# A two-layer transformer trunk in fp32: every down unit of the MLP by seven block products, added to the state unit by unit

## The chip, the cores and the metric

One NeuronCore of a Trainium2 chip runs the whole kernel as one launch. The metric is device time in microseconds (us): the median of several runs of one program. The engines run their own instruction streams in order and wait for each other through semaphores: TensorE (PE, matmuls into PSUM), VectorE (DVE) and ScalarE (ACT) for elementwise work, GpSimd (POOL) for slower elementwise work and for DMAs that add to their destination, SyncE (SP) for plain DMAs.

## The reference

The input x is 512 tokens by 1024 features. Two layers follow, each with a token mixer (attention), a squared-ReLU MLP and a gated per-layer embedding, and a norm at the end:

```python
def rmsnorm(x, g, eps=NORM_EPS):
    x32 = x.astype(jnp.float32)
    y = x32 * lax.rsqrt(jnp.mean(x32 * x32, axis=-1, keepdims=True) + eps) * g.astype(jnp.float32)
    return y.astype(x.dtype)
...
    for i in range(DEPTH):
        hn = rmsnorm(h, norm_mix_g[i])
        ...
        hn = rmsnorm(h, norm_mlp_g[i])
        u = jnp.square(jax.nn.relu(hn @ w_mlp_up[i]))
        h = h + u @ w_mlp_down[i]
        gate = jax.nn.sigmoid(rmsnorm(h, norm_ple_g[i]) @ w_ple_gate[i])
        h = h + (p[i] @ w_ple_proj[i]) * gate
    return rmsnorm(h, final_norm_g)
```

The change lies in the line `h = h + u @ w_mlp_down[i]` (4096 hidden features to 1024), and in the output at the very end.

## The kernel before, in words

The state h is kept transposed in SBUF as eight tiles of 128 features by 512 tokens, h[0] to h[7]. To keep fp32 accuracy, every factor of a matmul is split into a high part, rounded to the format fp32r, and a low part, the rest; a product is three matmuls (`mm3`): high by high, high by low, low by high (lines 138, 141, 142). The high part is a copy on ScalarE, the low part a subtraction on VectorE.

**Up blocks.** `up(ch, c)` (L711) computes 256 of the 4096 hidden features: two PSUM banks, 48 matmuls of 512 columns. From each it makes relu (L731), square (L732) and the seven sums of token and feature quarters that the products need (L737 to L741), and splits these as one tile of 128 x 1792: high part `uh` on ScalarE (L743), low part `ul` on VectorE (L744). The hidden features are worked in four chunks (NCH), each of four up blocks.

**Down units.** `down(ch, c)` (L755) multiplies one chunk (1024 hidden features) by the weights of 256 output features, the tiles h[2c] and h[2c+1]. It is a Strassen-like scheme: seven products of weight combinations with the hidden combinations, where eight would be plain. Each product is four k steps of three matmuls of 256 columns, so a unit is 84 matmuls. The weights come as four blocks A12, A22, A21, A11 of 128 x 512 (1024 KB in `raw`, two buffers). Their sums are s13 = (A21 + A22, A21 + A11) and s24 = (s13 + A11, that + A12), by VectorE (L768 to L773); in the last chunk s13 is made by two plain DMAs and one adding DMA on GpSimd (`add_up`, L749). `split` (L775) takes high and low parts into the buffers `wh` and `wl` (three of each) and, for the single block A11, into the small buffers `e`.

Of its four banks a unit adds one and a half to the state (L828, L830). The other products are summed over the chunks in tiles of their own, `sides` (copied in the first chunk, added by VectorE at L809 in the next two, added by a DMA from GpSimd at L803 in the last), and `side_sums` (L858) folds them into the state with eight additions of 128 x 256 once per output pair, in the last chunk.

**The last unit** of each layer, `down_last` (L834), is plain: for each of its two output tiles eight k steps, of which four are two matmuls of 256 columns and four one matmul of 512, times three. Before it in the program, in the last chunk, `up` makes an extra hidden tile `b12` for it (L735, L736).

**The order of the work.** Per chunk ch = 1 to 3: up(ch, 0), then down(ch-1, 0 to 3), then up(ch, 1 to 3). After that come the last chunk's units, down(3, 0 to 3). Since down(3, 0) needs the tile of up(3, 3), which is just done, its first k steps 0 to 2 are dealt ahead of k step 3: before, for its first four products (L818). When a state tile is final, `nxt.done` (L234) splits it, times the next norm's gains (L182, L183), and adds its square to a running sum (L241, L249). A scheduler fixes the order of each engine's stream from the program and its dependencies; `order(later, earlier)` adds a constraint.

**The end.** `ple_final` (L910) transposes the state back by 32 transposes on TensorE (L920), in the program ahead of the gate's products (`contract`, L945).

In the mixers GpSimd makes the low parts of weights (L126, two halves of each tile); in the MLP VectorE does (L128, and `split`).

## Time and profile before

| | |
|---|---|
| median of 3 runs | 1308.12 us |
| lowest, highest | 1306.33, 1308.19 us |
| the profiled execution: time, span | 1309.71, 1307.9 us |
| TensorE's granted clock, mean | 0.995 |
| TensorE busy | 1279.3 us (98%) |
| VectorE busy | 1005.4 us (77%) |
| ScalarE busy | 711.8 us (54%) |
| GpSimd busy | 212.0 us (16%) |
| DMA moved | 144.25 MB, mean 110 GB/s |

How to read the profile: it is one execution, and all its times are from that one. A row of a group says line, engine, operation, tile written <- tiles read, shape and count, then busy time and mean ns of one, then the idle time of that engine ahead of these instructions and what ended it. In a timeline the first number is the start and the second the length, both in us. "PE mm L138 <- ACT uh L743: 3.9, 2, 2.2" in the waits says: TensorE's matmuls of line 138 waited for ScalarE's `uh` of line 743 for 3.9 us in all, twice, at most 2.2 us. A windows row gives the window, its length and then for each engine the busy time with the count of instructions. A DMA row ends with KB and the median us from issue to landing.

### The profile page before, as it was taken

Reading aid. Unit: us, or ns where it says so; the run is one execution under the profiler, and the core shown is the slowest. Engines: PE = TensorE matmul, PEld = TensorE weight load, DVE = VectorE, ACT = ScalarE, POOL = GpSimd, SP = SyncE. Lnnn points to the kernel's source line nnn. Section 1 sums busy time; section 2 is a strip of 40 time slices with the busy share of each in tenths; the row PEclk is TensorE's granted clock in tenths of the full one; section 3 lists DMA queues with packets and bytes.
Section 4 is the critical chain, followed back from the end, with each engine's and each line's share of the span. In section 5 each row is a group of like instructions: output and inputs, shape, how many; then the busy total and the mean of one; then the engine's idle time right before and its main releaser. Section 6 shows DMA issues by size and latency. Waiting matters only on the chain.

```text
span 1307.9 us, 19332 instructions
## 1 busy us (share of the span) xinstructions
PE 1279.3 (98%) x7520; PEld 1128.1 (86%) x7520; DVE 1005.4 (77%) x1673; ACT 711.8 (54%) x1149; POOL 212.0 (16%) x184
## 2 busy tenths in 40 slices
PE   9999999999999999999999999999999999999997
PEld 7988787888998989989889888788899898997976
DVE  6788888778848869679767777887785885986876
ACT  5666768555534335355456666765553433534544
POOL 2433434310000000001024333222000000000201
PEclk9999999999999999999999999999999999999999
DMA  6421423223232222647432222212223123254741
GB/s 210 142 81 50 134 92 122 86 77 120 68 127 97 97 97 97 193 107 187 166 124 86 81 89 81 65 57 97 97 97 128 66 100 127 77 170 137 173 146 65
DMA packets 33995, 144.25 MB, mean 110 GB/s; under 512 B 3888, under 2 KB 4624, under 8 KB 21232
## 3 DMA queue, kind: packets, MB, share of 16 engines
q1 hardware_dynamic: 29680, 135.16, 30.5%
q0 software_dynamic: 4224, 7.87, 3.5%
q8 instruction: 59, 0.97, 0.3%
q14 instruction: 32, 0.26, 0.1%
HBM read 131.92 MB, written 6.37 MB: 106 GB/s over the span
## 4 chain that ended last, share of the span: by engine, by line
PE 78%; DVE 11%; ACT 6%; DMA 3%; issue 2%; SPq 0%; POOL 0%; ACTq 0%; DVEq 0%; POOLq 0%
PE mm L138 10%; PE mm L141 10%; PE mm L142 10%; PE sc L141 5%; PE sc L142 5%; PE sc L138 5%; PE pv L142 4%; PE pv L141 4%; PE pv L138 4%; PE tp L142 4%; PE tp L141 4%; PE tp L138 4%; PE pv L553 2%; PE tp L534 2%; DMA raw<-in_w_down_dram 1%
## 5 line engine op out<-in xcount | busy, mean ns | idle before, releaser
L122 ACT ACTIVATE wh<-raw 128x1024 fp32r<-128x1024 f32 (+1 forms) x156 | 160.6, 1034 | 146.5 <-PE mm L141 50.7
L126 POOL TENSOR_TENSOR wl<-raw,wh 128x512 fp32r<-128x512 f32 (+1 forms) x132 | 177.1, 1364 | 311.0 <-ACT wh L122 294.8
L138 PE MATMUL mm<-hi,wh 128*128 128x512 f32 x472 | 187.4, 397 | 0.6 <-DVE v L445 0.4
L142 PE MATMUL mm<-hi,wl 128*128 128x512 f32 x472 | 185.0, 392 | 0.1
L141 PE MATMUL mm<-lo,wh 128*128 128x512 f32 x472 | 185.1, 392 | 0.0
L128 DVE TENSOR_TENSOR wl<-raw,wh 128x1024 fp32r<-128x1024 f32 x90 | 109.7, 1221 | 46.4 <-ACT wh L122 40.8
L142 PEld LDWEIGHTS mm<-hi,wl 128*128 128x128 f32 x472 | 88.9, 188 | 20.1 <-POOL wl L126 0.5
L138 PEld LDWEIGHTS mm<-hi,wh 128*128 128x128 f32 x472 | 89.0, 188 | 17.2 <-DVE v L445 0.6
L141 PEld LDWEIGHTS mm<-lo,wh 128*128 128x128 f32 x472 | 89.1, 189 | 15.7
L753 POOL DMA_DIRECT2D s<-in_w_down_dram x4 | 4.5, 1123 | 579.3 <-DMA s<-in_w_down_dram 313.8
L528 ACT ACTIVATE e<-e,mn 128x128 f32<-128x128 f32 (+3 forms) x96 | 53.8, 561 | 65.9 <-DVE mn L525 65.5
L782 ACT ACTIVATE wh<-s 128x1024 fp32r<-128x1024 f32 x58 | 61.1, 1053 | 52.0 <-DVE s L769 14.7
L744 DVE TENSOR_TENSOR ul<-u,uh 128x1792 fp32r<-128x1792 f32 x32 | 64.8, 2024 | 30.2 <-ACT uh L743 30.1
L743 ACT ACTIVATE uh<-u 128x1792 fp32r<-128x1792 f32 x32 | 54.5, 1702 | 48.3 <-DVE u L741 48.3
L783 DVE TENSOR_TENSOR wl<-s,wh 128x1024 fp32r<-128x1024 f32 x58 | 70.8, 1221 | 12.8 <-ACT wh L782 12.3
L732 ACT ACTIVATE u<-u 128x512 f32<-128x512 f32 x64 | 39.7, 626 | 67.9 <-DVE u L731 67.6
L138 PE MATMUL sc<-hi,wh 128*128 128x512 f32 x184 | 72.0, 391 | 0.7 <-ACT hi L182 0.7
L141 PE MATMUL sc<-lo,wh 128*128 128x512 f32 x184 | 72.0, 392 | 0.6 <-DVE lo L183 0.6
L142 PE MATMUL sc<-hi,wl 128*128 128x512 f32 x184 | 71.8, 390 | 0.0
L138 PE MATMUL mm<-wh,hi 128*128 128x256 f32 (+1 forms) x216 | 63.2, 292 | 0.0
L142 PE MATMUL mm<-wh,lo 128*128 128x256 f32 (+1 forms) x216 | 63.0, 292 | 0.0
L141 PE MATMUL mm<-wl,hi 128*128 128x256 f32 (+1 forms) x216 | 62.8, 291 | 0.0
(303 smaller groups left out, 3891.8 us busy)
## 6 DMA issues: line engine op xcount, KB each, us to landing
raw<-in_w_up_dram SPq DMA_DIRECT2D x32, 1024.0 KB, 4.8
raw<-in_w_down_dram SPq DMA_DIRECT2D x32, 1024.0 KB, 4.8
raw<-in_w_in_dram SPq DMA_DIRECT2D x23, 1024.0 KB, 4.9
raw<-in_w_gate_dram SPq DMA_DIRECT2D x8, 1024.0 KB, 6.1
bias<-urow SPq DMA_DIRECT2D x24, 256.0 KB, 3.8
raw<-in_w_outa_dram SPq DMA_DIRECT2D x8, 768.0 KB, 4.2
pj<-pjd SPq DMA_DIRECT2D x16, 256.0 KB, 5.3
h<-in_xT_dram SPq DMA_DIRECT2D x8, 256.0 KB, 6.0
```

The costliest lines, as they stand in the source:

```text
L122: nc.scalar.activation(hi, src, AF.Copy)
L126: nc.gpsimd.tensor_tensor(lo[:, kx], src[:, kx], hi[:, kx].bitcast(F32), op=ALU.subtract)
L128: nc.vector.tensor_tensor(lo, src, hi.bitcast(F32), op=ALU.subtract)
L138: mm = nc.tensor.matmul(acc, lh, rh, start=start, stop=False)
L141: nc.tensor.matmul(acc, lh, rl, start=False, stop=False)
L142: nc.tensor.matmul(acc, ll, rh, start=False, stop=stop)
L528: nc.scalar.activation(e[:, 0:n], e[:, 0:n], AF.Exp, scale=-1.0, bias=mn, accum_out=s)
L732: nc.scalar.activation(ui, ui, AF.Square, scale=0.5)
L743: nc.scalar.activation(uh, u, AF.Copy)
L744: part = nc.vector.tensor_tensor(ul, u, uh.bitcast(F32), op=ALU.subtract)
L782: nc.scalar.activation(hi, src, AF.Copy)
L783: low[:] = [nc.vector.tensor_tensor(lo, src, hi.bitcast(F32), op=ALU.subtract).ins]
```

## The change

Every down unit, the last of a layer included, now runs the seven products, and each adds its results to the state itself; the side tiles, `b12`, `down_last`, `finished` and `side_sums` are gone. The block order in memory becomes A12, A22, A11, A21. In every unit s13 is made by two plain DMAs and an adding DMA, the raw load brings three blocks (768 KB), and GpSimd makes S2 = s13[0] + A11 and s4 = S2 + A12 (one 128 x 512 addition each). Three tiles of 128 x 1024 are split, and s4 in `e` tiles. The results come in four banks: ScalarE copies the first (L783), and eight VectorE additions (L794 to L802), four of 512 and four of 256 columns, put everything into h[2c] and h[2c+1]. In the last chunk's first unit all seven products do k steps 0 to 2 before k step 3. In the final stage the transposes are a function of the half, `turn(0)` and `turn(1)`, called after the products of blocks 1 and 2.

```diff
         def up(ch, c):
...
-            part = nc.vector.tensor_tensor(ul, u, uh.bitcast(F32), op=ALU.subtract)
-            hidden[ch, c] = (uh, ul, part.ins)
-
-        A12, A22, A21, A11 = range(4)
+            nc.vector.tensor_tensor(ul, u, uh.bitcast(F32), op=ALU.subtract)
+            hidden[ch, c] = (uh, ul, t4.ins)
+
+        A12, A22, A11, A21 = range(4)
+        S2 = A21
+
+        def halves(src, pool, tag, bufs):
+            n = src.shape[1]
+            hi, lo = (pool.tile([P, n, 4, P], F32R, tag=t, name=nm(t), bufs=b) for t, b in zip(tag, bufs))
+            src = src.rearrange("p s (k c) -> p s k c", k=4)
+            nc.scalar.activation(hi, src, AF.Copy)
+            return hi, lo, nc.vector.tensor_tensor(lo, src, hi.bitcast(F32), op=ALU.subtract).ins
+
+        def factors(src, late=None):
             sv = src.rearrange("p (s c) -> p s c", s=4)
+            s13 = fpool.tile([P, 2, S], F32, tag="s13", name=nm("s13"), bufs=2)
             for x in range(2):
                 nc.sync.dma_start(s13[:, x], sv[:, A21])
-            nc.gpsimd.dma_start(s13, sv[:, A22:A11 + 1:2], accum_op=ALU.add)
...
+            nc.gpsimd.dma_start(s13, sv[:, A22:A11 + 1], accum_op=ALU.add)
+            raw = wpool.tile([P, 4, S], F32, tag="raw", name=nm("raw"), bufs=2)
+            nc.sync.dma_start(raw[:, 0:3], sv[:, 0:3])
+            s4 = fpool.tile([P, 1, S], F32, tag="s4", name=nm("s4"), bufs=1)
+            nc.gpsimd.tensor_tensor(raw[:, S2], s13[:, 0], raw[:, A11], op=ALU.add)
+            nc.gpsimd.tensor_tensor(s4[:, 0], raw[:, S2], raw[:, A12], op=ALU.add)
+            w = ("wh", "wl")
+            w13 = halves(s13, wpool, w, (3, 3))
+            w12 = halves(raw[:, A11:S2 + 1], wpool, w, (3, 3))
+            wa2 = halves(raw[:, A12:A22 + 1], wpool, w, (3, 3))
+            w4 = halves(s4, spool, ("e", "e"), (T_BUFS["e"],) * 2)
+            if late is not None:
+                order(wa2[2], late)
+                order(w4[2], late)
+            return [(w12, 0, B11), (w13, 0, T1), (w12, 1, T2), (w13, 1, T3), (wa2, 0, B21), (w4, 0, B22), (wa2, 1, T4)]
+
+        def products(ws, us, head=False):
             banks = [ps_wide() for _ in range(4)]
-
-            def product(bank, half, w, x, t, start, stop, ks=range(4)):
-                wh, wl = w
+            t = spool.tile([P, S], F32, tag="e", name=nm("xw"), bufs=T_BUFS["e"])
+            places = [(0, 0), (0, 1), (1, 0), (1, 1), (2, 0), (2, 1), (3, 0)]
...
+            for ks in ((0, 1, 2), (3,)) if head else (range(4),):
+                for p in (0, 1, 3, 2, 4, 5, 6):
+                    product(p, ks)
+            nc.scalar.activation(t, banks[0], AF.Copy)
+            return banks, t
+
+        def down(ch, c):
+            last = ch == NCH - 1
+            head = last and c == 0
+            ws = factors(w_down[layer, 4 * ch + c], hidden[ch, 3][2] if head else None)
+            banks, t = products(ws, [hidden[ch, k] for k in range(4)], head)
+            left, right = slice(0, HW), slice(HW, S)
+            h1, h2 = h[2 * c], h[2 * c + 1]
+            x, w = t[:, left], t[:, right]
+            nc.vector.tensor_tensor(h1, h1, banks[0], op=ALU.add)
+            nc.vector.tensor_tensor(t, t, banks[1], op=ALU.add)
+            nc.vector.tensor_tensor(h2[:, left], h2[:, left], banks[1][:, right], op=ALU.subtract)
+            nc.vector.tensor_tensor(h1[:, right], h1[:, right], x, op=ALU.add)
+            h2v = h2.rearrange("p (a c) -> p a c", a=2)
+            nc.vector.tensor_tensor(h2v, h2v, t[:, None, left].to_broadcast([P, 2, HW]), op=ALU.subtract)
+            nc.vector.tensor_tensor(h2[:, right], h2[:, right], w, op=ALU.subtract)
+            nc.vector.tensor_tensor(h1, h1, banks[2], op=ALU.add)
+            nc.vector.tensor_tensor(h2[:, left], h2[:, left], banks[3][:, left], op=ALU.subtract)
             if last:
...
+                for i in range(2):
+                    nxt.done(2 * c + i)
...
-        side_sums(3)
-        for c in range(3):
+        for c in range(4):
             down(NCH - 1, c)
-        down_last(3)
...
                     if b == 1:
+                        turn(0)
+                    if b == 2:
                         rcol = tok_cols(norm.finish())
+                        turn(1)
```

What this makes of VectorE's stream where the first down unit of a chunk ends and the second begins (third round of layer 0). Before: `ul` (L744) is the hidden tile's low part, `wl` and `e` (L783) are low parts of weights, L809 adds to a side tile, L828 and L830 to the state.

```order
L744 TENSOR_TENSOR ul_4944<-u_4941,uh_4943 128x1792
L783 TENSOR_TENSOR wl_5085<-s_913_5074,wh_5084 128x1024
L828 TENSOR_TENSOR h_93<-h_93,tp_4966 128x512
L830 TENSOR_TENSOR h_94<-h_94,tp_4967 128x256
L783 TENSOR_TENSOR wl_5089<-s_914_5075,wh_5088 128x1024
L783 TENSOR_TENSOR wl_5159<-raw_5072,wh_5158 128x1024
```

The second unit's first low part stands ahead of the two state additions of the first unit, its second low part behind them. After, at the same place (L730 is now the hidden tile's low part, L741 a weight's, L794 to L802 add to the state):

```order
L730 TENSOR_TENSOR ul_4991<-u_4989,uh_4990 128x1792
L795 TENSOR_TENSOR xw_5030<-xw_5030,sc_5027 128x512
L796 TENSOR_TENSOR h_94<-h_94,sc_5027 128x256
L797 TENSOR_TENSOR h_93<-h_93,xw_5030 128x256
L799 TENSOR_TENSOR h_94<-h_94,xw_5030 128x512
L801 TENSOR_TENSOR h_93<-h_93,tp_5028 128x512
L800 TENSOR_TENSOR h_94<-h_94,xw_5030 128x256
L802 TENSOR_TENSOR h_94<-h_94,tp_5029 128x256
L741 TENSOR_TENSOR wl_5134<-s_912_5124,wh_5133 128x1024
L741 TENSOR_TENSOR wl_5138<-raw_5128,wh_5137 128x1024
L741 TENSOR_TENSOR wl_5142<-raw_5128,wh_5141 128x1024
```

All three wide low parts of the second unit now stand behind the last state addition of the first, which reads the bank `tp_5029` of the first unit's last product. TensorE's stream at the same place, after (pv_5149 to mm_5152 are the second unit's banks):

```order
L138 MATMUL pv_5149<-uh_4210,wh_5137 128x256
L141 MATMUL pv_5149<-ul_4211,wh_5137 128x256
L138 MATMUL pv_5150<-uh_4210,wh_5133 128x256
L141 MATMUL pv_5150<-ul_4211,wh_5133 128x256
L138 MATMUL mm_5151<-uh_4210,wh_5141 128x256
L141 MATMUL mm_5151<-ul_4211,wh_5141 128x256
L138 MATMUL mm_5152<-uh_4210,wh_5141 128x256
L141 MATMUL mm_5152<-ul_4211,wh_5141 128x256
L142 MATMUL pv_5150<-uh_4210,wl_5134 128x256
```

Eight matmuls that need only high parts come first, and the ninth reads the low part `wl_5134`. In the last chunk of layer 0, where its first unit ends and its second begins, VectorE's stream before (L865 folds a side tile, L183 is the low part of a final state tile, L773 makes a weight sum):

```order
L783 TENSOR_TENSOR wl_5785<-stage_5482,wh_5784 128x1024
L828 TENSOR_TENSOR h_93<-h_93,sc_5666 128x512
L830 TENSOR_TENSOR h_94<-h_94,sc_5667 128x256
L783 TENSOR_TENSOR wl_5789<-s_1006_5777,wh_5788 128x1024
L783 TENSOR_TENSOR wl_5861<-raw_5775,wh_5860 128x1024
L865 TENSOR_TENSOR h_93<-h_93,side_3068 128x256
```

The second unit's weights are split ahead of the folding. After:

```order
L800 TENSOR_TENSOR h_94<-h_94,xw_5738 128x256
L802 TENSOR_TENSOR h_94<-h_94,sc_5737 128x256
L741 TENSOR_TENSOR wl_5855<-s_1012_5845,wh_5854 128x1024
L183 SCALAR_TENSOR_TENSOR lo_5833<-h_93,gcols,hi_5832 128x512
L183 SCALAR_TENSOR_TENSOR lo_5839<-h_94,gcols,hi_5838 128x512
L249 TENSOR_TENSOR rstd_5836<-rstd_5836,e_5842 128x512
L741 TENSOR_TENSOR wl_5859<-raw_5849,wh_5858 128x1024
L741 TENSOR_TENSOR wl_5863<-raw_5849,wh_5862 128x1024
```

Behind the eight state additions stands the first low part, then the two state tiles' low parts and the square sum, and only then the second.

More of the change, by code (lines that the diff above doesn't have):

```diff
@@ L707, in mlp @@
         NCH = 4
-        sides = [[fpool.tile([P, S], F32, tag=f"side{x}{c}", name=nm("side"), bufs=1) for x in range(2)] for c in range(4)]
-        hidden, spare, stages, b12, low, lows = {}, [], [], [], [], []
+        hidden = {}
         def up(ch, c):
@@ L805, in total @@
-            def total(x, bank):
-                if ch == 0:
-                    nc.scalar.activation(sides[c][x], banks[bank], AF.Copy)
-                elif not last:
-                    nc.vector.tensor_tensor(sides[c][x], sides[c][x], banks[bank], op=ALU.add)
-                else:
-                    collect(sides[c][x], banks[bank])
-            w13, w24 = split(s13), split(s24)
-            lows.append(low[0])
-            w11 = split(rv[:, A11:A11 + 1])
-            if last and c == 0:
-                lows.clear()
@@ L853, in finished @@
[L853 to L867 removed]
+                    uh, ul = us[k][:2]
@@ L913, in ple_final, with turn @@
         ahl = norm.parts()
-        hk = []
-        for t in range(QT):
-            ht = fpool.tile([P, D], F32, tag=f"ht{t}", name=nm("ht"), bufs=1)
-            for c in range(2):
+        hk = [fpool.tile([P, D], F32, tag=f"ht{t}", name=nm("ht"), bufs=1) for t in range(QT)]
+        def turn(c):
+            for t, ht in enumerate(hk):
                 tp = ps("tp")
```

113 lines of the change are left out of this document (9 added, 104 removed).

## The prediction, made before the changed kernel was run

> **What bounds the kernel now.** I read the page first, then the windows of the layer 0 MLP, then TensorE's waits, then the timeline between two down units. A measurement of this kernel tells about 0.2% (2.6 us) from no change.
>
> ```profile
> span 1307.9 us, 19332 instructions
> PE 1279.3 (98%) x7520; PEld 1128.1 (86%) x7520; DVE 1005.4 (77%) x1673; ACT 711.8 (54%) x1149; POOL 212.0 (16%) x184
> ...
> PE 78%; DVE 11%; ACT 6%; DMA 3%; issue 2%; SPq 0%; POOL 0%; ACTq 0%; DVEq 0%; POOLq 0%
> ```
>
> ```profile
> 266.00:560.00 294.00, 294.00 (x1775) 264.03 (x1774) 224.29 (x291) 132.47 (x151) 4.22 (x4) 1.00 0.33 108
> 560.00:602.00 42.00, 39.98 (x273) 36.82 (x273) 35.31 (x51) 23.37 (x31) 5.91 (x7) 1.00 0.55 136
> ```
>
> ```profile
> PE mm L138 <- ACT uh L743: 3.9, 2, 2.2
> ...
> PE tp L920 <- DVE h L850: 1.8, 1, 1.8
> ```
>
> TensorE sets the time. From 266 to 560 us, which is layer 0's up blocks and its first three chunks of down units, it is busy for 294.00 of 294 us. There is nothing to win there except by fewer matmuls, and whatever makes TensorE wait there is lost in full. The idle that this change can reach is the 3.9 us, one wait per layer for the last hidden tile ahead of the last chunk, and the 1.8 us ahead of the final transposes.
>
> **What is removed: matmuls and two waits.** The first window holds one down unit (84 matmuls of 256 columns and two that overlap its edges), the second an up block (48 of 512 columns, likewise).
>
> ```profile
> 418.04:428.01 9.97, 9.97 (x86) 1.00 0.31 106
> ...
> 400.03:410.92 10.89, 10.89 (x50) 1.00 0.28 96
> ```
>
> So a matmul issues every 9.97/84 = 0.119 us or 10.89/48 = 0.227 us. The plain last unit, 48 narrow and 24 wide matmuls, takes 5.70 + 5.45 = 11.15 us; with seven products it takes 9.97. Twice 1.18 is 2.4 us saved.
>
> The first unit of the last chunk now does its first three k steps for seven products instead of four, before it needs the last hidden tile: 63 matmuls, 7.5 us of cover where there were 36, 4.3 us. Before, the wait was 3.9/2 = 1.95 us a layer; 3.2 us more cover takes it. Late next are that tile's low part and the low part of the unit's own weights, both within a microsecond of their cover by the durations below, so I take all 3.9 and keep 0 to 3.9. The transposes are dealt out behind products that don't need the last state tile; I take 1.8 (0 to 1.8, if the gate weights are late instead). Sum of gains: 2.4 + 3.9 + 1.8 = **8.1 us**.
>
> **What is moved: the state additions.** Before, a unit added two results to the state and put the rest in side sums; the order shown with the change has them, and the weight splits of the next unit around them. This is one such transition on VectorE, with ScalarE's first split of the next unit (that unit starts on TensorE at 428.01, the one after at 437.99):
>
> ```profile
> 421.20 0.68 DVE L809 TENSOR_TENSOR side<-side,sc 128x512 f32<-128x512 f32 x1
> 421.80 0.42 DVE L741 SCALAR_TENSOR_TENSOR u<-u 128x256 f32<-128x256 f32 x1
> ...
> 424.49 2.02 DVE L744 TENSOR_TENSOR ul<-u,uh 128x1792 fp32r<-128x1792 f32 x1
> 426.43 1.22 DVE L783 TENSOR_TENSOR wl<-s,wh 128x1024 fp32r<-128x1024 f32 x1
> 427.56 0.68 DVE L828 TENSOR_TENSOR h<-h,tp 128x512 f32<-128x512 f32 x1
> 428.21 0.42 DVE L830 TENSOR_TENSOR h<-h,tp 128x256 f32<-128x256 f32 x1
> 428.55 1.22 DVE L783 TENSOR_TENSOR wl<-s,wh 128x1024 fp32r<-128x1024 f32 x1
> 429.68 1.22 DVE L783 TENSOR_TENSOR wl<-raw,wh 128x1024 fp32r<-128x1024 f32 x1
> ```
>
> ```profile
> 437.99 0.28 PE L138 MATMUL sc<-uh,wh 128*128 128x256 f32 x1
> ```
>
> ```profile
> 438.13 1.06 ACT L782 ACTIVATE wh<-raw 128x1024 fp32r<-128x1024 f32 x1 [0.70 <-PE mm L141]
> ```
>
> Three things are to be seen. VectorE takes 0.60 us from one 512-wide operation to the next, 0.34 for 256, 1.13 for 1024, 1.94 for 1792. An addition that needs a unit's last matmul starts 0.20 us after that unit's end. And before, the first low part that the next unit needs (426.43) stands ahead of that addition, so TensorE never sees it. In the changed order the low parts of both weight tiles with which the second unit of a chunk begins stand **behind** the last state addition of the first unit. Eight matmuls (0.95 us) are all that TensorE can do without them.
>
> The floor is read off the rows: the addition runs at 0.20 after the unit's end, 0.34 later the split starts, 1.22 later it is done, at 1.76; less 0.95 is **0.8 us** of stall, with VectorE free of backlog.
>
> It is not free. The durations for the other steps:
>
> ```profile
> L782 ACT ACTIVATE wh<-s 128x1024 fp32r<-128x1024 f32 x58 | 61.1, 1053 | 52.0 <-DVE s L769 14.7 <-PE sc L141 14.3 <-PE tp L141 8.7
> L743 ACT ACTIVATE uh<-u 128x1792 fp32r<-128x1792 f32 x32 | 54.5, 1702 | 48.3 <-DVE u L741 48.3
> L732 ACT ACTIVATE u<-u 128x512 f32<-128x512 f32 x64 | 39.7, 626 | 67.9 <-DVE u L731 67.6
> L182 ACT ACTIVATE hi<-h,gcols 128x512 fp32r<-128x512 f32 x48 | 33.6, 715 | 26.9 <-DVE h L850 8.0 <-DVE h L690 7.6 <-DVE h L865 7.0
> L183 DVE SCALAR_TENSOR_TENSOR lo<-h,gcols,hi 128x512 fp32r<-128x512 f32 x48 | 35.1, 746 | 5.8 <-ACT hi L182 5.7
> ```
>
> Count from the first unit's start; it ends at 9.97. The preceding up block's relu, square and sums leave VectorE at about 3.7, ScalarE copies the unit's bank (0.6), splits the small factor (0.6) and then the hidden tile (1.7) until 5.9, and VectorE's low part of that tile, which stands ahead of seven state additions, ends at 7.8. The seven take 3 x 0.60 + 4 x 0.34 = 3.2: the split behind them starts at 11.0 and is done at 12.2. TensorE could have used it at 9.97 + 0.95: **1.3 us** of stall. (ScalarE's split of the third weight tile, whose buffer comes free at the unit's end, is done at 9.97 + 0.14 + 1.06 = 11.2 and is inside this.) Of the later units one split stands ahead of the additions, and 19 matmuls (2.25 us) cover the 1.76 us of the other: 0, at most 0.5.
>
> **What is added: GpSimd's additions.** Nothing of before shows them in this place; the nearest rows are GpSimd's weight splits in the mixers:
>
> ```profile
> 261.33 2.54 POOL L126 TENSOR_TENSOR wl<-raw,wh 128x512 fp32r<-128x512 f32 x2 [3.72 <-ACT wh L122]
> ```
>
> ```profile
> 250.03 2.44 POOL L126 TENSOR_TENSOR wl<-raw,wh 128x384 fp32r<-128x384 f32 x2 [2.56 <-ACT wh L122]
> ```
>
> ```profile
> 250.24 1.34 DVE L597 TENSOR_TENSOR e<-e,e 128x511 f32<-128x511 f32 x1
> ```
>
> ```profile
> L597 DVE TENSOR_TENSOR e<-e,e x32: 279/662/1656, 150.2 to 250.2; 128x127 f32<-128x127 f32 x8, 128x255 f32<-128x255 f32 x8, 128x383 f32<-128x383 f32 x8, 128x511 f32<-128x511 f32 x8
> ```
>
> Two additions take 2.54 us on GpSimd. A VectorE operation of 512 elements with both inputs in SBUF takes 1.34, at most 1.66, beside such work, instead of 0.68. The third unit's raw weights can be fetched only when the first unit's third weight tile is split (about 2.2), and need:
>
> ```profile
> raw<-in_w_outa_dram SPq DMA_DIRECT2D x8, 768.0 KB, 4.2
> ...
> s<-in_w_down_dram SPq DMA_DIRECT2D x8, 256.0 KB, 4.0
> s<-in_w_down_dram POOLq DMA_DIRECT2D x4, 512.0 KB, 7.2
> ```
>
> So the additions run from 6.4 to 9 or later, beside the low part and the state additions that make the 1.3 us. They cost between nothing and their whole 2.54: I take 1.0, one operation held up by 0.66 to 0.98 as in the rows. Per chunk then 1.3 + 1.0 + 0.2 for the later units = 2.5 (0.8 to 4.3); six chunks, **15 us** (5 to 26). The chain of the adding DMA (4.0 + 7.2) and two additions, 13.7 us, starts more than 20 us ahead of its use; I cost it at nothing, and if VectorE frees those buffers a unit later it shows.
>
> The Trainium skill, page "SBUF — State Buffer", section "Who interferes with whom", says that VectorE with two SBUF inputs and GpSimd hold a common port exclusively, each for its whole instruction. The 1.34 us is less than that gives (0.68 behind the rest of a 1.2 us addition), the 1.66 us about as much; by the rule my 1.0 would be 1.3 to 2.5.
>
> **The last chunk.** With the k steps dealt so, all four banks of its first unit close in the last 21 matmuls. Counted from that unit's end: bank copy until -1.0, eight additions until 2.8, low part of the first weight tile 2.8 to 4.0. Then stand the low parts of two finished state tiles (0.75 each) and a square sum (0.6), until 6.05, and only then the low part of the second weight tile, until 7.3. TensorE has eight matmuls before the first and twelve between the two, 2.4 us: stall 7.3 - 2.4 = **4.9 us** per layer. GpSimd's additions and the later units add 0 to 2.5; I take 0.9. Two layers: **11.6 us** (9.8 to 15).
>
> **Sum.** 15 + 11.6 - 8.1 = +18.5 us on the profiled 1309.71, thus 1328.2. The median of the runs is 1308.12, 1.6 below that execution, so I predict 1326.6.
>
> **The rivals.**
> (a) VectorE has no backlog and GpSimd disturbs nothing: six times 0.8, twice 4.9, less 8.1 is +6.5, to some +12 with the 1.3 of the timeline: 1315 to 1320. For it: VectorE is idle 23% of the span. Against it: the splits of the hidden tile stand in the same stretch.
> (b) GpSimd's additions hold VectorE for their whole length, always. VectorE's load per down unit is 4 x 0.60 + 4 x 0.34 for the state, 3 x 1.13 + 0.60 for splits, 7.8 us; with 2.54 it is 10.3, over TensorE's 9.97, and in four units back to back 1.4 us is lost in each of eight chunks: +11 on my sum, 1338, and up to 1342. For it: the 1.66 us row. Against it: five of the eight additions read PSUM, and have one SBUF input only. This is the rule of the Trainium skill's page "SBUF — State Buffer" at its worst.
> (c) Faster: the stalls together stay under the 8.1 us of gains. This decides if TensorE gets the low parts before its 0.95 us runs out, which needs the state additions done within the unit; with none left it is 1300.0. For it: TensorE takes 84 matmuls to do, and VectorE's load is under its time. Against it: the order, and the last addition's need of the last matmul; even the floors exceed the gains.
>
> **How the numbers follow.** Forecast (+13 to +27) 0.52, (a) 0.18, (b) 0.12, (c) 0.15, and 0.03 for gains and stalls that cancel. Range: (a)'s whole span and the gap below it, down to 1306, and to 1338, which takes in the lower half of (b); most of (c) and the top of (b) are left out, some 2 in 10. Faster by over 0.2%: 0.15; within: 0.03; slower: 0.82.
>
> **What would show it.** In the changed profile TensorE's waits should name the low parts of L741 at the second unit of each chunk, 1 to 4 us each, largest in the two last chunks (5 to 7); VectorE should be running state additions (L794 to L802) when they occur; waits for the hidden tile and ahead of the transposes should be gone. If L741 doesn't appear among the waits, the forecast is wrong and (c) right; if waits are for GpSimd's sums or for DMAs, I have costed the fetch chain wrongly.

## The result and the profile after

The changed kernel is slower: 1358.86 us median of four runs (1357.21 to 1359.31) against 1307.40 of before (1306.33 to 1308.19), a ratio of 1.0392 [1.0374, 1.0410]. The forecast was 1326.6 (1306 to 1338): right in its sign, far too small in its size. The profiled execution took 1358.43 us with a mean granted clock of 0.985; before 1309.71 and 0.995.

The page:

```profile
span 1356.4 us, 19725 instructions
PE 1294.1 (95%) x7544; PEld 1138.1 (84%) x7544; DVE 1030.8 (76%) x1663; ACT 707.4 (52%) x1149; POOL 322.9 (24%) x256
```

GpSimd is busy for 111 us more. TensorE was busy 98% of the span and is now 95%, and its busy time is 15 us longer although it has less to do: the granted clock, below, shows why.

TensorE's waits (us in total, times, longest):

```profile
PE pv L142 <- DVE wl L741: 16.0, 6, 2.7
PE sc L142 <- DVE wl L741: 8.3, 11, 1.1
PE tp L142 <- DVE wl L741: 4.5, 5, 1.4
PE mm L138 <- ACT wh L740: 3.3, 6, 0.6
```

The named wait came: the low parts of the weights, L741. The six of 2.7 us are the second units of the six chunks that are not the last of a layer. The wait for the last hidden tile, 3.9 us before, is gone; but in its place the first unit of each layer's last chunk now waits for a weight's low part, 1.04 us in layer 0 and 1.03 in layer 1:

```profile
600.17 0.38 PE L142 MATMUL sc<-uh,wl 128*128 128x256 f32 x1 [1.04 <-DVE wl L741]
```

One second unit, in TensorE's timeline. The first unit's matmuls end at about 345.3.

```profile
346.50 0.39 PE L138 MATMUL mm<-uh,wh 128*128 128x256 f32 x1 [0.56 <-ACT wh L740]
...
349.89 0.39 PE L142 MATMUL pv<-uh,wl 128*128 128x256 f32 x1 [2.65 <-DVE wl L741]
...
350.38 0.42 PE L142 MATMUL pv<-uh,wl 128*128 128x256 f32 x1
350.59 0.42 PE L138 MATMUL pv<-uh,wh 128*128 128x256 f32 x1
```

Two things are to be seen: the stall of 2.65 us, and that behind it a matmul starts every 0.21 us instead of every 0.12. The windows show why (the first number behind the counts is the granted clock):

```profile
347.00:350.00 3.00, 0.35 (x4) 0.14 (x3) 3.00 (x6) 0.00 (x0) 0.00 (x0) 1.00 0.00 0
350.00:353.50 3.50, 3.50 (x18) 3.50 (x19) 2.11 (x2) 0.00 (x0) 0.00 (x0) 0.54 0.66 137
353.50:357.00 3.50, 3.50 (x31) 3.50 (x30) 0.52 (x1) 1.62 (x3) 0.87 (x1) 0.97 0.82 254
```

For some 3.4 us behind the stall TensorE gets half its clock: 18 matmuls where some 29 fit (3.5 / 0.119). That costs another 1.7 us.

VectorE at the same place, from the up block's sums to the split that TensorE waits for:

```profile
326.76 1.78 DVE L723 TENSOR_TENSOR u<-u 128x512 f32<-128x512 f32 x1
328.58 1.39 DVE L725 SCALAR_TENSOR_TENSOR u<-u 128x256 f32<-128x256 f32 x1
...
342.31 2.03 DVE L730 TENSOR_TENSOR ul<-u,uh 128x1792 fp32r<-128x1792 f32 x1 [0.63 <-ACT uh L729]
...
345.18 0.58 DVE L797 TENSOR_TENSOR h<-h,xw 128x256 f32<-128x256 f32 x1
345.68 1.76 DVE L799 TENSOR_TENSOR h<-h,xw 128x512 f32<-128x512 f32 x1
347.36 0.67 DVE L801 TENSOR_TENSOR h<-h,tp 128x512 f32<-128x512 f32 x1
...
348.30 0.41 DVE L802 TENSOR_TENSOR h<-h,tp 128x256 f32<-128x256 f32 x1
348.63 1.21 DVE L741 TENSOR_TENSOR wl<-s,wh 128x1024 fp32r<-128x1024 f32 x1
```

And GpSimd's two additions, for two units:

```profile
326.11 1.88 POOL L753 TENSOR_TENSOR raw<-s,raw 128x512 f32<-128x512 f32 x1 [8.88 <-DMA raw<-in_w_down_dram]
328.07 1.62 POOL L754 TENSOR_TENSOR s<-raw 128x512 f32<-128x512 f32 x1
...
343.46 2.02 POOL L753 TENSOR_TENSOR raw<-s,raw 128x512 f32<-128x512 f32 x1 [10.54 <-DMA raw<-in_w_down_dram]
345.56 1.33 POOL L754 TENSOR_TENSOR s<-raw 128x512 f32<-128x512 f32 x1
```

Where a VectorE operation with two SBUF inputs starts while an addition runs on GpSimd, it is long: L723 1.78, L725 1.39, L799 1.76 us, while L801, which reads PSUM, keeps its 0.67. The additions meet VectorE twice per chunk, in the up block and in the first unit, and the split starts at 348.63 instead of at about 345.4.

**Where the 48.5 us of span lie.** Sums over TensorE's timelines, of each distance between matmul starts above 0.119 us (256 columns) or 0.227 us (512), by place:

| | before | after | difference | forecast |
|---|---|---|---|---|
| matmuls saved | | | -2.4 | -2.4 |
| gaps in the chunks and last units | 5.2 | 41.1 | +35.9 | +22.7 |
| half clock (0.21 instead of 0.12 us) | 2.9 | 14.9 | +12.0 | 0 |
| final stage | 60.8 | 64.4 | +3.6 | -1.8 |
| sum | | | +49.1 | +18.5 |

The parts are 0.6 us more than the difference of the spans; that rest was not placed. Of the 41.1 the second units of six chunks have 21.2, the two last chunks 13.0, the later units 2.7, and the first units of three chunks, for which nothing was forecast, 3.4; 0.8 lie elsewhere.

In the final stage the wait ahead of the transposes has gone, and others have come: 0.35, 1.11 and 0.73 us, 2.2 us in all, for the transposes' evacuation and the gate weights. Before had 1.78 and, for a gate weight, 0.68. So TensorE waits no longer than before, and the +3.6 us lie elsewhere: behind its last matmul, which is, before and after,

```profile
1299.08 0.28 PE L142 MATMUL mm<-wh,lo 128*128 128x256 f32 x1
```

```profile
1343.64 0.28 PE L142 MATMUL mm<-wh,lo 128*128 128x256 f32 x1
```

From there to the end of the span are 8.8 us before and 12.8 after: the elementwise work of the output stands later.

### The profile page after: what moved, and what is told of

Read it like the earlier page. It is cut to its first block, busy times and chain, and to the rows that moved or that the text cites. A ratio compares the mean times of both kernels' runs of the same rounds, so it can differ in the third digit from the quotient of the medians.

```text
span 1356.4 us, 19725 instructions
## 1 busy us (share of the span) xinstructions
PE 1294.1 (95%) x7544; PEld 1138.1 (84%) x7544; DVE 1030.8 (76%) x1663; ACT 707.4 (52%) x1149; POOL 322.9 (24%) x256
## 5 line engine op out<-in xcount | busy, mean ns | idle before, releaser
L122 ACT ACTIVATE wh<-raw 128x1024 fp32r<-128x1024 f32 (+1 forms) x152 | 156.3, 1033 | 151.6 <-PE sc L141 52.5
L753 POOL TENSOR_TENSOR raw<-s,raw 128x512 f32<-128x512 f32 x32 | 52.7, 1648 | 421.1 <-DMA raw<-in_w_down_dram 197.5
L128 DVE TENSOR_TENSOR wl<-raw,wh 128x1024 fp32r<-128x1024 f32 x86 | 105.3, 1236 | 41.0 <-ACT wh L122 36.5
L730 DVE TENSOR_TENSOR ul<-u,uh 128x1792 fp32r<-128x1792 f32 x32 | 65.5, 2046 | 41.9 <-ACT uh L729 41.7
L740 ACT ACTIVATE wh<-raw 128x1024 fp32r<-128x1024 f32 x64 | 67.1, 1051 | 45.1 <-PE tp L141 19.9
L741 DVE TENSOR_TENSOR wl<-raw,wh 128x1024 fp32r<-128x1024 f32 x64 | 82.3, 1310 | 6.7 <-ACT wh L740 6.7
L740 ACT ACTIVATE wh<-s 128x1024 fp32r<-128x1024 f32 x32 | 33.7, 1053 | 94.6 <-PE pv L141 56.2
L142 PE MATMUL pv<-uh,wl 128*128 128x256 f32 x224 | 67.1, 309 | 16.0 <-DVE wl L741 16.0
L741 DVE TENSOR_TENSOR wl<-s,wh 128x1024 fp32r<-128x1024 f32 x32 | 39.7, 1240 | 49.7 <-ACT wh L740 49.7
```

Source lines behind the costliest of these rows:

```text
L122: nc.scalar.activation(hi, src, AF.Copy)
L128: nc.vector.tensor_tensor(lo, src, hi.bitcast(F32), op=ALU.subtract)
L142: nc.tensor.matmul(acc, ll, rh, start=False, stop=stop)
L730: nc.vector.tensor_tensor(ul, u, uh.bitcast(F32), op=ALU.subtract)
L740: nc.scalar.activation(hi, src, AF.Copy)
L741: return hi, lo, nc.vector.tensor_tensor(lo, src, hi.bitcast(F32), op=ALU.subtract).ins
```

## The experiments

Theory A: two costs are added, the low parts that stand behind the state additions on VectorE, and GpSimd's additions, which hold VectorE up whenever both read SBUF; and the stalls bring stretches at half clock on top. Its rivals are named in the expectations. All medians are set against runs of before on the same chip.

**1. The final transposes as before** (`e1_turn_back`). Only the two-part transposes are undone:

```diff
-        def turn(c):
-            for t, ht in enumerate(hk):
...
+        for t in range(QT):
...
+            for c in range(2):
...
```

> The changed kernel with the final stage's transposes as before (all of them in the program ahead of the gate's products, the norm finished after block 1); everything else as changed. In the changed profile the final stage, from the last down matmul to the end of the span, takes 64.4 us against 60.8 before. Theory: dealing out the transposes delays the norm's columns and so the epilogue of the first half, which then stands in the tail. Then this gives back 3 to 5 us: about 1354 to 1356, with a final stage of 60 to 62 us. Rival: the longer final stage comes from how the last down unit ends (its two state tiles become final together, so the gate's weights are split later), and putting the transposes back changes it by less than 1 us.

1356.65 us, 1.0359 [1.0337, 1.0381]. This interval overlaps that of the changed kernel, so the times alone don't tell the two apart. In the profile the final stage, last down matmul to end, takes 61.5 us instead of 64.4, and the tail behind the last matmul is 8.6 us again instead of 12.8. So the two parts cost 2 to 3 us by the profile; they were forecast to win 1.8. **The counterpart** (`e8_before_turns`) adds the two-part transposes alone to the kernel before:

> The kernel before with only the final transposes dealt out in two parts as in the change. Nothing is left out. Theory A (the dealing out finishes the norm's columns later and lengthens the tail by more than the 1.8 us wait that it removes): slower by 1 to 4 us, 1309 to 1312. Rival: the wait goes and nothing else moves: 1306 to 1307.

1310.79 us, 1.0014 [1.0004, 1.0024], 1.8 us slower. The wait for the last state tile doesn't go (2.6 us in two waits, where before had 1.8 in one), and the tail behind the last matmul is 12.4 us for 8.8. Both agree: the dealing out moves work behind the last matmul.

**2. No additions on GpSimd** (`e2_no_gpsimd_adds`). The order stays:

```diff
-            nc.sync.dma_start(raw[:, 0:3], sv[:, 0:3])
+            nc.sync.dma_start(raw, sv)
...
-            nc.gpsimd.tensor_tensor(raw[:, S2], s13[:, 0], raw[:, A11], op=ALU.add)
-            nc.gpsimd.tensor_tensor(s4[:, 0], raw[:, S2], raw[:, A12], op=ALU.add)
+            nc.sync.dma_start(s4[:, 0], sv[:, A12])
```

> The changed kernel without GpSimd's two additions per unit: S2 and s4 are loaded as blocks A21 and A12 instead (which leaves part of the weight sums out, so the product is another). The order on VectorE and TensorE stays as changed. Theory A (order, and on top of it GpSimd's additions holding up VectorE): the waits at the first unit of a chunk (1.2 to 1.3 us, five times) go, those at the second fall from 3.5 to 1.3 to 1.8 us, and with them most of the stretches at half clock (12 us in all): 1322 to 1336. Theory B (the order alone, with VectorE's backlog as it is, makes the waits; GpSimd's additions cost little): the second unit's wait stays above 3 us, 1350 to 1358.

1329.16 us, 1.0145 [1.0119, 1.0171]. VectorE's timeline, at the places shown above:

```profile
325.84 0.69 DVE L723 TENSOR_TENSOR u<-u 128x512 f32<-128x512 f32 x1
326.56 0.42 DVE L725 SCALAR_TENSOR_TENSOR u<-u 128x256 f32<-128x256 f32 x1
...
345.40 1.22 DVE L741 TENSOR_TENSOR wl<-s,wh 128x1024 fp32r<-128x1024 f32 x1
```

The long operations are short (0.69 for 1.78, 0.42 for 1.39), and the second unit's gaps are 0.7 and 0.3 us. Some 30 us of the slowdown hang on the two additions. What is left, 19 us, is not all the order's. The edit brings a stall of its own: s4 is now loaded into a tile with one buffer, the load comes late, ScalarE waits for it, and the high part that stands behind it on ScalarE keeps TensorE waiting at the fourth unit (ScalarE, then TensorE):

```profile
453.82 0.63 ACT L740 ACTIVATE e<-s 128x512 fp32r<-128x512 f32 x1 [4.82 <-DMA s<-in_w_down_dram]
```

```profile
455.45 0.39 PE L138 MATMUL mm<-uh,wh 128*128 128x256 f32 x1 [2.01 <-ACT wh L740]
```

There are five such waits, up to 2.76 us and 7.7 us in all, and two of them are followed by half clock. An estimate from these rows: 10 to 11 us of this execution's 23 over before come from the late load, so that the order, the clock behind its own stalls and the final stage have less than the 19 us.

**3. The next unit's splits ahead of the state additions** (`e3_splits_ahead`). GpSimd's additions stay:

```diff
...
+            if c < 3:
+                ahead.append(factors(w_down[layer, 4 * ch + c + 1]))
...
+            if c < 3:
+                order(adds[0].ins, ahead[0][1][0][2])
+                order(adds[1].ins, ahead[0][0][0][2])
```

> The changed kernel with the next unit's weight fetch and splits written ahead of a unit's state additions, and the first two of these additions ordered behind the next unit's first two low parts. Nothing is left out. Theory A: the waits for L741 at the second units go (29 us in eight chunks) and with them the half clock (12 us); what is left are the first units' waits by GpSimd's additions (5.8 us), and the final stage's 3.6: 1314 to 1326. Theory C (VectorE with GpSimd's contention is simply too full, so a wait taken from one place comes back at another, at the state's banks or the next split): above 1340.

1341.45 us, 1.0255 [1.0229, 1.0280]. Outside A's expectation, and such as the rival had it: the waits at the second units, which A said would go, are as long as ever (16.0 and 3.3 us in the changed kernel):

```profile
PE pv L142 <- DVE wl L741: 18.9, 6, 3.4
```

What the new order won lies in the two last chunks, in the later units and in the half clock, which takes five times 3.4 us where it took nine times in the changed kernel. **Both edits together** (`e4_both`):

> The two edits together: splits ahead of the state additions, and no GpSimd additions (part of the weight sums left out). Theory A: no waits of more than 0.5 us in the chunks, full clock: 1306 to 1312 (the final stage's 3.6 us stay, against 2.4 us of matmuls and 3.9 us of head waits gained). Theory C: VectorE was too full because of GpSimd; also near 1310. If it stays over 1320, something else than these two makes the waits.

1307.89 us, 0.9993 [0.9983, 1.0003]: the same as before. The four kernels are a table of two by two (those of the right column leave part of the weight sums out):

| | GpSimd adds | no additions |
|---|---|---|
| state additions first | 1.0392 | 1.0145 |
| splits first | 1.0255 | 0.9993 |

The additions cost 0.025 to 0.026 (32 to 34 us) in either order, the order 0.014 to 0.015 (18 to 20 us) with or without them. So both costs of A are there. That they simply add isn't shown: the differences agree in size but not in make-up. With the additions the order won next to nothing at the second units; without them it won the 6.2 us there, and by the estimate above about half of its 20 us are the late load of experiment 2. Why the second units' wait doesn't go away with the order is seen where their splits stand. VectorE and GpSimd of experiment 3:

```profile
344.48 2.31 DVE L741 TENSOR_TENSOR wl<-s,wh 128x1024 fp32r<-128x1024 f32 x1
346.71 2.28 DVE L741 TENSOR_TENSOR wl<-raw,wh 128x1024 fp32r<-128x1024 f32 x1
```

```profile
343.52 2.18 POOL L753 TENSOR_TENSOR raw<-s,raw 128x512 f32<-128x512 f32 x1 [10.49 <-DMA raw<-in_w_down_dram]
345.79 2.12 POOL L754 TENSOR_TENSOR s<-raw 128x512 f32<-128x512 f32 x1
```

VectorE in experiment 4:

```profile
341.88 1.22 DVE L741 TENSOR_TENSOR wl<-s,wh 128x1024 fp32r<-128x1024 f32 x1
343.01 1.22 DVE L741 TENSOR_TENSOR wl<-raw,wh 128x1024 fp32r<-128x1024 f32 x1
```

The splits grow from 1.22 to 2.31 and 2.28 us, by about one addition each (half the pair's 2.54), and the recorded additions to 2.18 and 2.12: the engines take turns, each instruction waiting for the other's whole one. The Trainium skill, page "SBUF — State Buffer", section "Who interferes with whom", calls it an exclusive lock on a shared pair of ports, held for the whole instruction; these rows agree with it.

**4. Additions that nobody reads** (`e7_useless_adds`). Are the additions late, or do they only disturb? Experiment 4 with two idle ones:

```diff
+            idle = fpool.tile([P, 2, S], F32, tag="idle", name=nm("idle"), bufs=1)
+            nc.gpsimd.tensor_tensor(idle[:, 0], s13[:, 0], raw[:, A11], op=ALU.add)
+            nc.gpsimd.tensor_tensor(idle[:, 1], idle[:, 0], raw[:, A12], op=ALU.add)
```

> The kernel with splits ahead and without GpSimd's sums (S2 and s4 loaded as blocks, so part of the weight sums is left out; 1307.9 us), and with two additions of 128 x 512 on GpSimd per unit put back, of the same inputs and at the same time, into a tile that nobody reads. Theory A (the two engines hold each other up at their inputs): the waits come back without anyone needing a result: 1334 to 1343, as with splits ahead and real sums (1341.5). Rival D (the sums came too late for the splits; VectorE's long operations were only waiting for data): 1307 to 1311.

1336.85 us, 1.0213 [1.0194, 1.0233]: 29 us for results that nothing waits for. GpSimd, then VectorE:

```profile
342.99 1.43 POOL L755 TENSOR_TENSOR idle<-s,raw 128x512 f32<-128x512 f32 x1 [9.99 <-DMA raw<-in_w_down_dram]
344.50 2.12 POOL L756 TENSOR_TENSOR idle<-idle,raw 128x512 f32<-128x512 f32 x1
```

```profile
343.18 2.33 DVE L741 TENSOR_TENSOR wl<-s,wh 128x1024 fp32r<-128x1024 f32 x1
345.43 2.28 DVE L741 TENSOR_TENSOR wl<-raw,wh 128x1024 fp32r<-128x1024 f32 x1
```

So the contention by itself explains most of the 32 to 34 us. Of the some 5 us that experiment 3 has more, 3 are seen at the first units, where TensorE waits for L741 for 4.5 us there and for 1.4 here; the rest is left open.

**5. GpSimd instructions that only write** (`e9_memsets`). Experiment 4 with four memsets in place of two additions:

```diff
+            nc.gpsimd.memset(raw[:, S2], 0.01)
+            nc.gpsimd.memset(raw[:, S2], 0.01)
+            nc.gpsimd.memset(s4[:, 0], 0.01)
+            nc.gpsimd.memset(s4[:, 0], 0.01)
```

> The kernel with splits ahead and without GpSimd's additions, with four GpSimd memsets of 128 x 512 per unit into S2 and s4 instead (so part of the weight sums is left out): GpSimd writes SBUF at the same times but reads nothing. Theory A, in the form that the engines meet at a shared read (as the Trainium skill's page SBUF - State Buffer has it for VectorE operations with two inputs): no hold-up, 1306 to 1311. Rival: any work of GpSimd in SBUF holds VectorE up: above 1320.

1310.76 us, 1.0028 [1.0017, 1.0039]. A memset and the split beside it:

```profile
342.21 0.53 POOL L754 MEMSET raw<- 128x512 f32 x1 [9.88 <-DMA raw<-in_w_down_dram]
```

```profile
342.69 1.22 DVE L741 TENSOR_TENSOR wl<-s,wh 128x1024 fp32r<-128x1024 f32 x1
```

The split keeps its 1.22 us. The same section of the Trainium skill's "SBUF — State Buffer" says that a VectorE instruction with two SBUF inputs contends with a GpSimd instruction that reads SBUF, not with one that only writes it; the rows agree. (Most of the 3 to 4 us left are two waits of TensorE for L741 in the last chunks, 2.9 us.)

**6. The sums made elsewhere.** Splits ahead, transposes as before, nothing left out. By adding DMAs (`e5_sums_by_dma`):

```diff
-            s4 = fpool.tile([P, 1, S], F32, tag="s4", name=nm("s4"), bufs=1)
-            nc.gpsimd.tensor_tensor(raw[:, S2], s13[:, 0], raw[:, A11], op=ALU.add)
-            nc.gpsimd.tensor_tensor(s4[:, 0], raw[:, S2], raw[:, A12], op=ALU.add)
+            nc.sync.dma_start(raw[:, S2], sv[:, A11])
+            s4 = fpool.tile([P, 1, S], F32, tag="s4", name=nm("s4"), bufs=2)
+            nc.sync.dma_start(s4[:, 0], sv[:, A12])
+            nc.gpsimd.dma_start(raw[:, S2], s13[:, 0], accum_op=ALU.add)
+            nc.gpsimd.dma_start(s4[:, 0], raw[:, S2], accum_op=ALU.add)
```

> Splits ahead of the state additions, the transposes as before, and S2 and s4 made by adding DMAs (A11 and A12 loaded, then s13's first half and S2 added to them from SBUF) instead of GpSimd additions. Nothing is left out. Theory A (GpSimd's additions hold up VectorE; the order does the rest): without additions on GpSimd the waits are gone: 1303 to 1309. Rival: the chain of two more adding DMAs in a row (some 5 us each) brings the sums too late, and TensorE waits for splits of S2 and s4: above 1315.

1391.19 us, 1.0627 [1.0605, 1.0649], the slowest of all, and the rival's case: three adding DMAs stand in a row.

```profile
s<-in_w_down_dram POOLq DMA_DIRECT2D x32, 512.0 KB, 8.1
...
raw<-s POOLq DMA_DIRECT2D x32, 256.0 KB, 5.0
s<-raw POOLq DMA_DIRECT2D x32, 256.0 KB, 4.6
```

8.1 + 5.0 + 4.6 = 17.7 us from issue to landing, behind the plain loads, and TensorE waits for high parts (L740) up to 5.7 us at a time. By VectorE (`e6_sums_by_vectore`, `nc.vector` for `nc.gpsimd` in both lines):

> The same with S2 and s4 added by VectorE. Nothing is left out. VectorE's load per down unit rises by 2 x 0.60 to 9.0 us, under TensorE's 9.97. Theory A: no contention, little room: 1305 to 1318. Theory C (VectorE has no room for what GpSimd was given): waits come back, above 1320, and GpSimd's additions were not the trouble in themselves.

1315.33 us, 1.0045 [1.0027, 1.0064]. It is the best version of the changed scheme that leaves nothing out, and still no match for before. What it lacks lies in the final stage: its last down matmul starts at 1246.4 us, that of before at 1246.9, but the final stage takes 67.2 us for 60.8, with waits of up to 2.9 us ahead of the transposes and 6.8 us at half clock. VectorE does both additions itself at 78% busy, and that is 26 us faster than experiment 3, where GpSimd spares it that work (and where the two-part transposes still stand, 2 to 3 us).

**7. Is the first unit's new head worth its 3.9 us?** (`e12_before_head`) The kernel before, with all seven products of the last chunk's first unit doing their first three k steps first:

```diff
...
+                if head:
+                    product(2, 1, w24, 1, B22, True, False, ks)
+                    product(2, 0, w, 0, B21, False, True, ks)
+                    product(3, 0, w, 1, T4, True, True, ks)
```

> The kernel before with one part of the change: in the last chunk's first unit all seven products do k steps 0 to 2 before k step 3. Nothing is left out. If this part of the prediction holds, the two waits for the last hidden tile (3.9 us, and the half clock behind the second, 1.7) go: 1302 to 1305. Rival: the splits that this unit now needs earlier are late, and the wait only changes its name: 1306 to 1309.

1310.55 us, 1.0021 [1.0009, 1.0032]: over both ranges, and nearer to the rival's. The wait changes its name, twice:

```profile
PE mm L141 <- DVE ul L744: 3.1, 2, 1.7
```

TensorE now waits 3.1 us for the hidden tile's low part instead of 3.9 for its high part, and 1.4 us for the next unit's high part. Alone, the head gains nothing. Where the 2 us over before lie the trace can't say: its execution was the slowest of ten, 1313.54 us, and waits 4.1 us for the last state tile ahead of the final transposes, where before had 1.8.

**8. The clock.** Does a stall of this length take half the clock for a while, whatever it comes from? Two tries with longer splits of the second unit in experiment 4 (`e10_wait_long`: three repeats of one low part, `e11_wait_short`: one):

```diff
...
+            for _ in range(again):
+                v = raw[:, A11:S2 + 1].rearrange("p s (k c) -> p s k c", k=4)
+                w12 = (w12[0], w12[1], nc.vector.tensor_tensor(w12[1], v, w12[0].bitcast(F32), op=ALU.subtract).ins)
...
```

> The kernel with splits ahead and no GpSimd additions (part of the weight sums left out; 1307.9 us, no waits in the chunks), in which VectorE makes the low part of the second unit's first weight tile four times over, in all eight chunks: about 3 us of wait for TensorE at each. Clock theory (after a wait of this length the granted clock is 0.5 for 3.4 us): the time grows by the waits plus some 1.7 us for each of them that is followed by it: 8 x 3 + 8 x 1.7 = 38, 1335 to 1350, and the clock shows 0.5 behind the waits. Rival (the half clock in the changed kernel had another cause, as the DMA traffic or GpSimd): the time grows by the waits alone, about 24 us, clock near 0.996.

> The same with the low part made twice: about 1 us of wait at each of the eight places. Clock theory: no stretch at half clock; the time grows by the waits, 6 to 9 us: 1313 to 1318. Rival (any wait costs clock): 1320 or more.

1319.48 us, 1.0092 [1.0077, 1.0107], and 1308.62, 1.0001 [0.9992, 1.0011]. The stalls that they were made for did not come (at most 0.4 us each, TensorE's order went round them), so they say nothing of the clock; the 11 us that the first costs were not taken apart. The place was then changed: in the kernel before, the high part of each layer's last hidden tile is copied once more (`e13_head_wait_1`) or three times more (`e14_head_wait_3`), which lengthens the wait for it, one in each layer and 3.9 us in all:

```diff
+            if (ch, c) == (3, 3):
+                nc.scalar.activation(uh, u, AF.Copy)
```

> The kernel before, with ScalarE's copy of the last hidden tile's high part (128 x 1792, 1.70 us) made twice, so that TensorE's wait for it grows from 1.9 to about 3.6 us in layer 0 and from 2.4 to about 4.1 in layer 1. Nothing is left out. In the kernel before, the granted clock stays at 1.00 behind the first and falls to 0.50 for 3.4 us behind the second. Clock theory: it falls behind both; the time grows by 2 x 1.7 of wait and 1.7 of half clock, 5.1 us: 1312.5 to 1314.5. Rival (the fall has another cause): layer 0 keeps 1.00, 3.4 us: 1311 to 1312.

> The same with the copy made four times: waits of about 7 and 7.5 us. Clock theory: clock 0.50 in both layers, for 3.4 to 6.8 us; the time grows by 10.2 of wait and 1.7 to 5 of half clock: 1320 to 1324. Rival: 1318 to 1319.

1314.70 us, 1.0051 [1.0035, 1.0067], and 1322.94, 1.0109 [1.0091, 1.0126]: over the rivals' ranges, the first 0.2 us over the clock theory's too, the second inside it. The profile of before has a wait of 1.71 us and one of 2.24, and they differ in what follows. TensorE's timeline, then its windows behind each:

```profile
581.38 0.50 PE L138 MATMUL mm<-uh,wh 128*128 128x256 f32 x2 [1.71 <-ACT uh L743]
```

```profile
1209.35 0.51 PE L138 MATMUL mm<-uh,wh 128*128 128x256 f32 x2 [2.24 <-ACT uh L743]
```

```profile
582.00:585.00 3.00, 2.74 (x23) 1.00 0.08 33
```

```profile
1210.50:1214.00 3.50, 3.50 (x18) 0.53 0.00 0
```

Behind 1.71 us the clock stays at 1.00; behind 2.24 it is 0.53 and 18 matmuls run where some 29 fit. With the one copy more, the first layer's wait (2.3 us, and 1.15 for the low part behind it) is followed by half clock as well:

```profile
584.00:587.00 3.00, 2.32 (x11) 0.50 0.00 0
```

So the half clock comes behind stalls, in before too, and is not a trait of the changed scheme. But the length of a stall doesn't settle it. Experiment 3 has two waits of 3.10 us at second units of layer 1; behind the first the clock stays, behind the second it falls:

```profile
992.03 0.39 PE L142 MATMUL pv<-uh,wl 128*128 128x256 f32 x1 [3.10 <-DVE wl L741]
...
1167.77 0.39 PE L142 MATMUL pv<-uh,wl 128*128 128x256 f32 x1 [3.10 <-DVE wl L741]
```

```profile
992.10:995.50 3.40, 3.40 (x29) 1.00 0.40 100
1168.10:1171.50 3.40, 3.40 (x18) 0.50 0.52 93
```

The traces show a pattern. In each of them the stretches at half clock start whole multiples of 3.41 us apart (in the changed kernel at 350.3, 439.0 and 531.2 us, 26 and 27 steps), and all but the last of each last one to three steps. On this grid the first wait of 3.10 us falls across two steps and fills about half of each; the second fills nine tenths of one. In all traces together, from 300 to 1285 us, every step at full clock in which TensorE was idle for 0.54 or more was followed by half clock (45 of 45), and of those under 0.40 none was; between the two it went either way (12 of 36). So what seems to count is the idle share of a step, and with it where a stall happens to fall; no run was made to test that. The Trainium skill, page "TensorE: Matmul & The Clock Gate", section "HAM oscillation — how this bites in real kernels", gives as its rule "no PE-idle gaps >~3.4µs". The length of the throttled stretch, some 3.4 us, is the window that this page has. The bound is not borne out here: a wait of 2.24 us was enough, and in the changed kernel 0.56 and 2.65 us with four matmuls between, though not each time (3.10 us, above).

## Why the prediction was right in its sign and wrong in its size

- **What bounds the kernel** was right: TensorE sets the time, and each stall cost at least its length.
- **Matmuls and the last hidden tile**: right for the matmuls, 2.4 us. Of the 3.9 us the prediction took all; the wait is gone under its name, but 2.1 us came back at the same units as waits for a weight's low part, one of the two that it had named as late next. That the head alone would have won it is wrong too (experiment 7): it pays only with what stands around it.
- **The order on VectorE**: right as a mechanism, and in size where GpSimd's work is left out: in experiment 2's timeline the second units lose 6.2 us, 1.03 a chunk, where the prediction had 0.8 and 1.3. That kernel as a whole is 19 us [16, 22] over before, and rival (a) gave 6.5 to 12; the rest is the late load of s4 with the half clock behind it, the half clock behind the last chunk, and the misjudged final stage. (With its own 1.3 us a chunk, (a) comes to 9.5 and not to 12.)
- **GpSimd's additions**: the step that failed, "I take 1.0, one operation held up by 0.66 to 0.98 as in the rows", six times. Instead each addition holds VectorE in turn with it, twice per chunk: L723 and L725 by 2.1 us, in the up block, which delayed the split of the hidden tile and cost the first units 3.4 us, and L797 and L799 by 1.2 us in the unit. The second units lose 21.2 us, forecast were 13.8; without the additions they lose 6.2, so there the additions cost 15 where 6 were put down. They also reach the later units (2.7 us, forecast 1.2) and the first units of the last chunks, and the added stalls then brought the clock. Taken out, the additions are worth 32 to 34 us. Rival (b) had the rule, "hold VectorE for their whole length, always", and at 1338 to 1342 too low a price, since it counted VectorE's load alone.
- **The argument against (b)**, "five of the eight additions read PSUM", is true of L801, which kept its 0.67 us, but the additions on GpSimd met the other operations: the up block's sums, and L797 and L799, which read SBUF only.
- **The clock** was in no step: a term put at nothing without a reason. The durations were taken at full clock; the stalls that the sum itself forecast, 2.3 us and more, were as long as the 2.24 us that had halved the clock in the trace of before. That costs 12.0 us, a quarter of the difference.
- **The last chunk**: 13.0 us measured for 11.6, which is near by luck. The second units lose 8.0 us where 9.8 were forecast, and about as much without GpSimd's additions (experiment 2); the first and the later units lose 5.0 where 1.8 were put down.
- **The two-part transposes**: wrong. Forecast -1.8, measured about +2 to +3, in two kernels (experiment 1). The prediction looked at the wait ahead of the transposes alone; the dealing out lengthened the tail behind the last matmul, by 4 us in the changed kernel. Of the final stage's +3.6 us the two parts are 2.9; the 0.7 left was not taken apart.

The range ended at 1338 because (b)'s upper half was left out; no case in it joined (b), the order and the clock, which is what happened. Of the signs it named, the wait for L741 at the second units came; that the longest would be in the two last chunks, 5 to 7 us, did not: no wait there is over 1.41 us.

## What to carry to other kernels

Count what a moved operation does to the engine that it stands beside, not only how long it takes: two additions of 512 columns on an engine that had 84% of its time free cost 32 us there, while the version that left them on the busier engine came within 0.45% of the kernel before. When an in-order engine feeds a bound one, look at what stands ahead of the operation that the bound engine needs next: splits before state additions were worth 18 us here, though the wait that they were moved for stayed until the additions were gone as well. A sum of short stalls on TensorE has to be costed with the half clock that may follow. And an edit that takes a suspect out can bring a wait of its own: look for new names among the waits before its time is put into a table.

## What the runs showed of the hardware that was not expected

- VectorE operations with two SBUF inputs and GpSimd additions took turns, instruction by instruction: 1.22 became 2.31 us for a 128x1024 subtraction beside a 128x512 addition of about 1.27. Beside memsets it stayed 1.22, and an addition that read PSUM stayed 0.67.
- TensorE's clock fell to half for some 3.4 us (half of which is lost, 1.7 us) behind waits of 2.24 us, and of 0.56 + 2.65 us with four matmuls between; behind 1.71 us it did not, and of two waits of 3.10 us it did behind one only. The half clock starts on a grid of 3.41 us steps, and steps idle for 0.54 or more were always followed by it.
- An adding DMA took 5.8 us (the changed kernel) to 8.1 us (experiment 6) for 512 KB and 4.6 to 5.0 us for 256 KB from issue to landing (medians), long enough there that three in a row were late.
